# One chain of 16 batches for the scan of four head pairs, with TensorE and loads in the source's order

## The chip, the cores and the metric

The kernel runs on one core of a Trainium2 chip. The metric is the device time of one execution in microseconds (us); a kernel's time is the median of its runs.

## The reference, cut to what matters

The reference is a two-layer trunk on 512 latent and 256 context tokens (768 together), width 1024. The first layer mixes by a recurrent scan (RWKV-7, in both directions) next to a windowed attention, the second by two attentions; each has an MLP behind it. Every sub-layer is modulated by a vector made from `c` and a large matrix `w_ada`. The change is in the scan and in that modulation:

```python
def rwkv7_scan(f, d, s0, reverse):
    def step(state, inp):
        r_t, w_t, k_t, v_t, kk_t, a_t = inp
        sa = jnp.einsum('bhvk,bhk->bhv', state, -kk_t)
        state = (state * w_t[:, :, None, :] + sa[..., None] * (kk_t * a_t)[:, :, None, :]
                 + v_t[..., None] * k_t[:, :, None, :])
        return state, jnp.einsum('bhvk,bhk->bhv', state, r_t)
...
        ml = jnp.split(s_lat @ w_ada[i] + b_ada[i], 6, axis=-1)
        mc = jnp.split(s_ctx @ w_ada[i] + b_ada[i], 6, axis=-1)
```

The scan has 8 heads of 64 and two directions `d`; a step's state is a 64 x 64 matrix for each head. Weights and activations are float32.

## The kernel before

The kernel treats the scan in chunks of 64 tokens, 12 chunks in each direction (`NCH`), and the 8 heads as 4 pairs `p`; both heads and both directions of a pair share each instruction's 128 partitions.

**Preparation.** `prep(p)` (L842) is a generator for one pair; each `yield` is a turn. It loads k and r, normalises (`heads_rstd`, L397), makes decays (L864 matmuls, L872 and L874 running sums), and stops at FRONT. Then it makes the factors `BK` and `AR` (L897 to L942) and a triangular matrix for each chunk (L911, L912), which goes through DRAM (`nscr`, L919, L922) into a layout in which VectorE inverts its 32 x 32 blocks by 31 rank-one updates (L948, L949: "the doubling" below); READY stands before these. The result goes through DRAM again (L953 to L961), MERGE stands there, and 192 small matmuls join the blocks (L968, L976) into `XI`. The tiles of pairs p and p+2 are the same buffers.

**The chain.** `chunks(p)` (L983) works on batches of `NB` = 3 chunks, four to a pair. For batch b: `factors` (transposes L1017, L1023, value matmuls L1031), `masked` (L1043, L1050), `own` (L1059), `solved` (L1068, which needs `XI`), `local` (L1080, L1093), `passed` (L1101 to L1107, giving MQ), and three `step`s (L1122, L1124, L1129), of which each needs the state of the one before. The loop at L1132 puts the first four of batch b between the last ones of batch b-1. A pair's chain is filled and drained on its own; it ends with the copy of `y` (L1158), which `mix_out` (L1161) turns into the pair's output.

**The modulation.** `ada` (L333) takes the 24 column blocks of `w_ada` of both layers; four are done earlier, 20 in this stage. A block is four loads of 512 KB (L341, three buffers), each used by 8 matmuls with 32-row stationary operands (L352, 16 instructions in the profile), then a copy to SBUF (L358), a summing transpose (L361) and an addition (L363).

**What sets the order.** For each pair the loop at L1468 takes the chain's turns; after each it takes `RATE3` turns of the background `behind` (the next pair's preparation, the previous pair's output, and the front of the pair after) and `RATE4` turns of `ada`:

```python
            for _ in cg:
                n += 1
                due[0] += RATE3
                due[1] += RATE4
                while due[0] >= 1:
                    due[0] -= 1
                    next(bg, None)
...
            for t in itertools.chain(bg, rest()):
                due[1] += RATE5
```

What is left of the background runs in `rest` before the next pair's chain begins. In this stage that is the order of the source only: a planner in the framework places every instruction on its engine by priority and by when it expects the operands, and so fixes each engine's queue before the program runs. The stage before (`tc.manual_schedule(engines=ORDERED)`, L1322) is one that keeps the source's order. PSUM is split here into two tiles of two banks (`wide`, for nearly everything), two banks for `y`, one for the state update `pd` and one for the modulation.

Of the kernel before, what the change touches and what calls it, by code (L numbers as in the profile page):

```python
# [28 lines left out]
RATE1, RATE2, RATE3, RATE4, RATE5 = 2.0, 1.5, 1.8, 0.7, 0.5  # L29
QUIET = "quiet"  # L30
FRONT = "front"
READY = "ready"
# [22 lines left out]
for _name, _w in [("ident", 128), ("bones", 128), ("cent", 128), ("ones", 1), ("bo2", 2), ("mab", 64), ("mr", 384), ("i2", 64),  # L55
                  ("mhalf", 12), ("sel", 8), ("tri", 256)]:
    CON[_name] = slice(_n, _n + _w)
    _n += _w
# [3 lines left out]
def constants():  # L62
# [12 lines left out]
    con[:, CON["mr"]] = np.concatenate([np.tile(s <= t, (1, 3)), np.tile(s + t <= 63, (1, 3))], 1)  # L75
# [12 lines left out]
    con[:, CON["sel"]] = (p[:, None] // 32 == np.arange(8)[None] // 2) & (p[:, None] % 32 == np.arange(8)[None] % 2)  # L88

# [86 lines left out]
def trunk(ctx: ExitStack, tc: tile.TileContext, xT, cT, vec_d, wada, we, wo_in, wout, wf1, wf2, lw2_d, la2_d, lg2_d,  # L176
# [188 lines left out]


# [30 lines left out]
    def heads_rstd(pl, x, n, ops, out, name="t0", bufs=2, **k):  # L397
# [3 lines left out]
        act(sq[:, :n], x, AF.Square, **k)  # L401
        pc = one()
# [6 lines left out]
        yield  # L409
        rx = pl.tile([128, 12, 64], F32, name=name, bufs=bufs)  # L410
        V.tensor_copy(rx[:, :2 * nt, :], r12[:, :2 * nt].unsqueeze(2).to_broadcast([128, 2 * nt, 64]))
        pb = wide()
# [429 lines left out]
    def prep(p, R, rt, iv, sts, res):  # L842
# [10 lines left out]
        yield from heads_rstd(rt, k, T, lambda o, i: ts(o, i, 1e-24, None, op0=ALU.max), pb, "t", NT0, scale=VV["kk"][:, p:p + 1])  # L853
# [88 lines left out]
        stt(kds, kds, VV["rk"][:, p:p + 1], r, op0=ALU.mult, op1=ALU.mult)  # L942
        yield READY
# [18 lines left out]
        res[p] = (AR, BK, XI, wc, kds)  # L962
# [20 lines left out]
    def chunks(p, y, ct, pch, res):  # L983
# [5 lines left out]
        AR, BK, XI, wc, kds = res[p]  # L989
# [3 lines left out]
        v = ct.tile([128, T], F32, name="v")  # L993
        nc.sync.dma_start(v, scr[3 + 3 * p + 2])
        py = pch.tile([128, 2, 512], F32, name="py")
        pd = pch.tile([128, 128], F32, name="pd")
        yp = py[:, :, 0:384].rearrange("p h (c f) -> p h c f", f=64)
        B = [{} for _ in range(NCH // NB)]
        last = None
        env = {}  # L1000

        def chain(*a, **k):

            nonlocal last
            if last is None:
                last = PE.matmul(*a, **k)
            else:
                with tc.issue_after(last.ins):
                    last = PE.matmul(*a, **k)  # L1009

        def factors(b):

            pt = wide()[:, 0:NB * 256].rearrange("p (x h k) -> p h x k", x=2 * NB, h=2)
            BT = B[b]["BT"] = ct.tile([128, 2, 2 * NB, 128], F32, name="BT", bufs=2)
# [4 lines left out]
            XA = B[b]["XA"] = ct.tile([128, NB, 2, 128], F32, name="XA", bufs=2)  # L1019
            pw = wide()  # L1020
# [3 lines left out]
            pv = pw[:, 512:512 + NB * 128].rearrange("p (i f) -> p i f", i=NB)  # L1024
            vr = ct.tile([128, NB, 64], F32, name="vr", bufs=2)
# [6 lines left out]
            act(XA[:, :, :, 64:128], pt)  # L1032
# [4 lines left out]
        def masked(b):  # L1037
# [412 lines left out]
    with ExitStack() as p2:  # L1450
# [9 lines left out]
        for t in early:  # L1460
            if t != QUIET:
                next(ag, None)
# [408 lines left out]
```

## Time and profile before

| | |
|---|---|
| time, median of 3 runs | 2070.47 us (2069.14 to 2079.63) |
| profiled execution | 2079.02 us, its span 2077.2 us |
| mean granted TensorE clock over the span | 0.964 |
| busy over the span: PE, PEld | 1940.1, 1663.0 us |
| busy over the span: DVE, ACT, POOL | 1116.6, 816.4, 115.2 us |

PE is TensorE's matmuls, PEld its loads of stationary operands, DVE VectorE, ACT ScalarE, POOL GpSimd, SPq the queue of SyncE, which issues most loads. Times in rows are microseconds from the span's start unless marked ns. The profiled execution is one of the kernel's executions and lies at the upper end of the runs. The granted clock is 1.0 or 0.5 (2.4 or 1.2 GHz) at each moment; a row shows its mean.

### The profile page before, as it was taken

How to read it: one execution, taken by the hardware profiler on the slowest of the kernel's cores; microseconds unless marked ns; L12 is line 12 of the kernel's file. 1: busy time of each engine (PE TensorE's matmuls, PEld its weight loads, DVE VectorE, ACT ScalarE, POOL GpSimd, SP SyncE). 2: the span in 40 equal slices, each digit the busy share in tenths (PEclk: the TensorE clock that was granted, in tenths of full speed). 3: DMA queues.
4: the chain of work that ended last, by engine and by line, in shares of the span. 5: the costliest groups of instructions: out<-in, count | busy, mean ns of one | idle time of the engine just before them, and what ended most of it. 6: DMA issues, size and time to landing. Idle time of an engine off the chain costs nothing.

```text
span 2077.2 us, 40236 instructions
## 1 busy us (share of the span) xinstructions
PE 1940.1 (93%) x17276; PEld 1663.0 (80%) x17276; DVE 1116.6 (54%) x1991; ACT 816.4 (39%) x1531; POOL 115.2 (6%) x129
## 2 busy tenths in 40 slices
PE   6999996889879899999999999899999899999997
PEld 4788774676667797888888889898878798888887
DVE  5576567546454468234443444765565566444445
ACT  3466432434325344413221232445686645322232
POOL 1000011001000000000000000001121000000000
PEclk9999997798979999999999999999999999999998
DMA  7421335575643234312221221333111425332221
GB/s 308 154 84 62 108 96 138 186 224 165 187 150 109 78 97 132 102 41 82 72 61 41 72 82 41 101 112 100 37 42 41 133 92 163 102 92 82 88 95 41
DMA packets 112019, 217.64 MB, mean 105 GB/s; under 512 B 38496, under 2 KB 63968, under 8 KB 111328
## 3 DMA queue, kind: packets, MB, share of 16 engines
q1 hardware_dynamic: 96544, 191.73, 29.3%
q10 hardware_dynamic: 15296, 23.33, 3.2%
q8 instruction: 135, 2.21, 0.5%
q14 instruction: 44, 0.36, 0.1%
HBM read 184.36 MB, written 28.05 MB: 102 GB/s over the span
## 4 chain that ended last, share of the span: by engine, by line
PE 73%; DVE 12%; issue 5%; ACT 4%; DMA 4%; POOL 2%; SPq 0%; POOLq 0%; ACTq 0%; DVEq 0%
PE x L1568 43%; PE x L429 11%; PE ax L529 3%; PE ax L510 2%; PE b L492 2%; PE b L493 1%; PE b L1009 1%; PE ad L352 1%; DVE X L949 1%; DMA w_raw<-in_wada_dram 1%; DVE pr L948 1%; PE b L1068 1%; DVE w_lo L226 1%; POOL r L265 1%; DMA w_raw<-in_wf_dram 1%
## 5 line engine op out<-in xcount | busy, mean ns | idle before, releaser
L183 ACT ACTIVATE w_hi<-w_raw 128x1024 fp32r<-128x1024 f32 x183 | 192.3, 1057 | 482.1 <-PE x L1568 361.0
L226 DVE TENSOR_TENSOR w_lo<-w_raw,w_hi 128x1024 fp32r<-128x1024 f32 x181 | 220.9, 1224 | 204.3 <-ACT w_hi L183 203.4
L1568 PE MATMUL x<-fl,w_hi 128*128 128x256 f32 (+1 forms) x864 | 291.6, 339 | 3.9 <-DVE fl L1655 3.9
L1568 PE MATMUL x<-fh,w_lo 128*128 128x256 f32 (+1 forms) x864 | 290.1, 337 | 0.0
L1568 PE MATMUL x<-uh,w_hi 128*128 128x512 f32 (+1 forms) x864 | 287.1, 338 | 3.0 <-ACT uh L183 2.9
L1568 PE MATMUL x<-ul,w_hi 128*128 128x512 f32 (+1 forms) x864 | 287.8, 336 | 0.0
L1568 PE MATMUL x<-uh,w_lo 128*128 128x512 f32 (+1 forms) x864 | 287.4, 335 | 0.0
L1568 PE MATMUL x<-fh,w_hi 128*128 128x256 f32 (+1 forms) x864 | 287.4, 338 | 0.0
L1582 DVE TENSOR_TENSOR oa<-x,oa 128x512 f32<-128x512 f32 (+1 forms) x184 | 103.1, 563 | 207.6 <-PE x L1568 206.9
L429 PE MATMUL x<-uh,w_hi 128*128 128x256 f32 (+1 forms) x560 | 189.6, 339 | 0.9 <-ACT po L183 0.6
L429 PE MATMUL x<-uh,w_lo 128*128 128x256 f32 (+1 forms) x560 | 188.3, 336 | 0.0
L429 PE MATMUL x<-ul,w_hi 128*128 128x256 f32 (+1 forms) x560 | 188.1, 336 | 0.0
L1568 PEld LDWEIGHTS x<-fl,w_hi 128*128 128x128 f32 x864 | 165.2, 191 | 22.0 <-DVE fl L1655 4.5
L1568 PEld LDWEIGHTS x<-fh,w_lo 128*128 128x128 f32 x864 | 164.9, 191 | 17.8
L1568 PEld LDWEIGHTS x<-uh,w_hi 128*128 128x128 f32 x864 | 161.9, 190 | 21.3 <-ACT uh L183 4.0
L1568 PEld LDWEIGHTS x<-fh,w_hi 128*128 128x128 f32 x864 | 162.7, 191 | 19.9 <-ACT fh L183 2.5
L1568 PEld LDWEIGHTS x<-ul,w_hi 128*128 128x128 f32 x864 | 162.7, 189 | 17.7
L1568 PEld LDWEIGHTS x<-uh,w_lo 128*128 128x128 f32 x864 | 162.7, 189 | 17.6
L429 PEld LDWEIGHTS x<-uh,w_hi 128*128 128x128 f32 x560 | 106.8, 191 | 10.1 <-ACT po L183 0.8
L429 PEld LDWEIGHTS x<-uh,w_lo 128*128 128x128 f32 x560 | 106.9, 191 | 9.7 <-issue 1.7
L429 PEld LDWEIGHTS x<-ul,w_hi 128*128 128x128 f32 x560 | 106.8, 191 | 9.1 <-issue 1.2
L1654 DVE TENSOR_TENSOR rl<-rl 128x512 f32<-128x512 f32 (+1 forms) x108 | 59.4, 551 | 72.2 <-ACT fh L183 72.0
(303 smaller groups left out, 3441.8 us busy)
## 6 DMA issues: line engine op xcount, KB each, us to landing
w_raw<-in_wf_dram SPq DMA_DIRECT2D x128, 512.0 KB
w_raw<-in_wada_dram SPq DMA_DIRECT2D x96, 512.0 KB
w_raw<-in_we_dram SPq DMA_DIRECT2D x21, 512.0 KB
w_raw<-in_wo_in_dram SPq DMA_DIRECT2D x18, 512.0 KB
w_raw<-in_wout_dram SPq DMA_DIRECT2D x16, 512.0 KB
hsc<-h ACTq DMA_DIRECT2D x8, 1024.0 KB
scr<-po ACTq DMA_DIRECT2D x21, 384.0 KB
h<-hsc SPq DMA_DIRECT2D x7, 1024.0 KB
```

The costliest lines, as they stand in the source:

```text
L183: return S.activation(o, i, f, **k)
L226: eng.tensor_tensor(o_lo, x, o_hi.bitcast(F32), op=ALU.subtract)
L265: G.tensor_tensor(dst, src, C["mhalf"][:, :n], op=ALU.pow)
L352: PE.matmul(ps[32 * j:32 * j + 32, 0:128], si[:, 2 * kp + k, :], w[:, k, j * 128:(j + 1) * 128], start=kp + k == 0, stop=kp == 3 and k == 1)
L429: PE.matmul(ps[:, 0:b - a], x, y, start=j == 0, stop=j == len(pairs) - 1)
L492: PE.matmul(ps[:, off:off + n], qs, kh, start=True, stop=False)
L493: PE.matmul(ps[:, off:off + n], qs, kl, start=False, stop=True)
L510: PE.transpose(pt[:, (kb - k0) * 128:(kb - k0 + 1) * 128], P[:, kb * 128:(kb + 1) * 128], ident)
L529: PE.matmul(po[h * 64:h * 64 + 64, 0:128], v(h, k), pts[h][:, k], start=k == 0, stop=k == n - 1)
L1568: PE.matmul(o, a, b, start=n == 0, stop=n == len(pairs) - 1)
L1582: tt(oa[:, m, tok], ps, oa[:, m, tok], op=ALU.add)
L1654: tt(r, r, r, op=ALU.mult)
```

## The change

The four chains become one generator `batches` over 16 batches g = 4p + b: in each iteration it works on batches g-1 (`given`, the steps), g (`begun`, `gained`, `passed`, first step) and g+1 (`factors`, `values`, `masked`, `own`, `solved`), also across the border of two pairs. `local` is cut in `gained` and `given`, `passed` in `begun` and `passed`, `factors` in `factors` and `values`. From the stage's `manual_schedule` on, TensorE and SyncE take their instructions in the source's order; the other engines are still planned. Three PSUM tiles of two banks serve everything but `y`; the state update and the modulation take theirs from them. `Ada` handles half blocks: four loads of 256 KB (six buffers) and one `run` of 16 matmuls, whose four 32-row bands keep the two k halves apart, and `turn` sums them with `sel4`. A run stands at each SIDE, two in an iteration, a `turn` at TURN. The background goes on by 1.4 turns after each named turn and is finished at MERGE, before the first `solved` of the next pair; six turns are added in `heads_rstd` of each preparation, and `mix_out` waits in its generator until its `y` is made.

```diff
-RATE1, RATE2, RATE3, RATE4, RATE5 = 2.0, 1.5, 1.8, 0.7, 0.5
+RATE1, RATE2, RATE3 = 2.0, 1.5, 1.4
...
+    class Ada:
+
+
+
+        def __init__(self, wa, which, eng):
+            self.wa, self.eng, self.got, self.rows = wa, eng, [], []
+            self.which = [(l, q, h) for l, q in which for h in range(2)]
+            self.todo = [wada[l, q, kp][:, :, 256 * h:256 * h + 256] for l, q, h in self.which for kp in range(4)]
+
+        def load(self, n):
+            while self.todo and len(self.got) < n:
+                w = self.wa.tile([128, 2, 256], F32, name="w_half")
+                self.eng.dma_start(w, self.todo.pop(0))
+                self.got.append(w)
+
+        def run(self, n):
+            if not self.which:
+                return
+            ps = wide()[:, 0:128]
+            for kp in range(4):
+                w = self.got.pop(0)
+                for k in range(2):
+                    for j in range(2):
+                        b = 32 * (2 * k + j)
+                        PE.matmul(ps[b:b + 32], si[:, 2 * kp + k, :], w[:, k, j * 128:(j + 1) * 128], start=kp == 0, stop=kp == 3)
+            self.load(n)
+            rows = sp.tile([128, 128], F32, name="adar", bufs=2)
+            act(rows, ps)
+            self.rows.append((rows, self.which.pop(0)))
+
+        def turn(self):
+            if not self.rows:
+                return
+            pt = wide()
+            for n, (rows, _) in enumerate(self.rows):
+                PE.matmul(pt[:, 4 * n:4 * n + 4], rows, C["sel4"], start=True, stop=True)
+            for n, (_, (l, q, h)) in enumerate(self.rows):
+                m = slice(4 * q + 2 * h, 4 * q + 2 * h + 2)
+                tt(mod[:, l, m, :], pt[:, 4 * n:4 * n + 4].rearrange("p (a b) -> p a b", b=2),
+                   VV[f"bada{l}"][:, m].unsqueeze(2).to_broadcast([128, 2, 2]), op=ALU.add)
+            self.rows = []
+
...
+        for _ in range(slow):
+            yield
         pc = one()
...
+        for _ in range(1 + slow):
+            yield
...
-        yield from heads_rstd(rt, k, T, lambda o, i: ts(o, i, 1e-24, None, op0=ALU.max), pb, "t", NT0, scale=VV["kk"][:, p:p + 1])
+        yield from heads_rstd(rt, k, T, lambda o, i: ts(o, i, 1e-24, None, op0=ALU.max), pb, "t", NT0, 2, scale=VV["kk"][:, p:p + 1])
...
-            pw = wide()
+            XA = B[g]["XA"] = ct.tile([128, NB, 2, 128], F32, name="XA", bufs=2)
+            pw = B[g]["pw"] = wide()
...
-            pv = pw[:, 512:512 + NB * 128].rearrange("p (i f) -> p i f", i=NB)
...
+            act(XA[:, :, :, 64:128], pt)
+            v = tile_of(g)["v"]
+            vr = B[g]["vr"] = ct.tile([128, NB, 64], F32, name="vr", bufs=2)
             c0 = BWD[NB * b + NB - 1]
             act(vr[:, ::-1, ::-1], c3(v)[:, c0:c0 + NB])
+
+        def values(g):
+            p, b = divmod(g, nb)
+            v, vr, pw = tile_of(g)["v"], B[g]["vr"], B[g]["pw"]
+            pv = pw[:, 512:512 + NB * 128].rearrange("p (i f) -> p i f", i=NB)
...
-            Z = B[b]["Z"] = ct.tile([128, NB, 2, 2, 64], F32, name="Z", bufs=2)
+            Z = B[g]["Z"] = ct.tile([128, NB, 2, 2, 64], F32, name="Z", bufs=2)
...
+            if b == nb - 1 and p < 3:
+                values_in(p + 1)
...
-            tt(B[b]["BT"][:, :, :, 64:128], pr, C["mr"].rearrange("p (x t) -> p x t", t=64).unsqueeze(1).to_broadcast([128, 2, 2 * NB, 64]), op=ALU.mult)
...
+            for d in range(2):
+                x = slice(d * NB, d * NB + NB)
+                tt(B[g]["BT"][:, :, x, 64:128], pr[:, :, x], C["mr"][:, 64 * d:64 * d + 64].unsqueeze(1).unsqueeze(1).to_broadcast([128, 2, NB, 64]), op=ALU.mult)
...
+            BT, Z = B[g]["BT"], B[g]["Z"]
+            b = g % nb
+            if not b:
+                py = pch.tile([128, 2, 512], F32, name="py")
+                tile_of(g)["y"] = py[:, :, 0:384].rearrange("p h (c f) -> p h c f", f=64)
+            yp = tile_of(g)["y"]
...
+        def begun(g):
+
+            p, b = divmod(g, nb)
+            AR = res[p][0]
             i0 = 0 if b else 1
             pm = wide().rearrange("p (d x) -> p d x", d=2)[:, :, 0:NB * 128].rearrange("p d (i k) -> p d i k", i=NB)
             for d in range(2):
-                chain(pm[:, d, i0:, 0:64], ident, C["i2"].unsqueeze(1).to_broadcast([128, NB - i0, 64]), start=True, stop=False)
-                chain(pm[:, d, i0:, 64:128], ident, AR[:, NB * b + i0:NB * b + NB, 2 + d], start=False, stop=False)
+                PE.matmul(pm[:, d, i0:, 0:64], ident, C["i2"].unsqueeze(1).to_broadcast([128, NB - i0, 64]), start=True, stop=False)
+                PE.matmul(pm[:, d, i0:, 64:128], ident, AR[:, NB * b + i0:NB * b + NB, 2 + d], start=False, stop=False)
+            B[g]["pm"] = pm
...
+            MQ = B[g]["MQ"] = ct.tile([128, 2, NB, 128], F32, name="MQ", bufs=2)
...
             if s < NCH - 1:
+                pd = wide()[:, 0:128]
...
+            if s == NCH - 1:
+                act(y.rearrange("p c (h f) -> p h c f", h=2), yp)
+                done_y.append(g // nb)
+
+        values_in(0)
+        for g in range(-1, 4 * nb + 1):
+            old, now, new = 0 < g, 0 <= g < 4 * nb, g + 1 < 4 * nb
+            work = [old and (given, g - 1), new and (factors, g + 1), now and (begun, g), TURN, new and (values, g + 1), now and (gained, g),
+                    new and (masked, g + 1), now and (passed, g), SIDE, new and (own, g + 1),
+                    old and (step, g - 1, 1), SIDE, old and (step, g - 1, 2), new and (solved, g + 1), now and (step, g, 0)]
+            for w in filter(None, work):
+                if w in (SIDE, TURN):
+                    yield w
+                    continue
+                if w[0] is solved and not w[1] % nb:
+                    yield MERGE
+                w[0](*w[1:])
+                yield (w[0].__name__, w[1])
...
-        sts[1], ct, tl, wa = side("st1"), side("ct"), side("tl"), side("wa", 3)
-        p2.enter_context(psum(0, 2))
+        sts[1], ct, tl, wa = side("st1"), side("ct"), side("tl"), side("wa", WH)
+        p2.enter_context(psum(0, 3))
         pch = p2.enter_context(pool("pch", 1, space=PSUM))
-        pad = p2.enter_context(pool("pad", 1, space=PSUM))
-        mk = lambda: pad.tile([128, 512], F32, name="ad")
-        ag = ada(wa, 3, mk, [(0, q) for q in range(4, 12)] + [(1, q) for q in range(12)], nc.sync)
+        ag = Ada(wa, [(0, q) for q in range(4, 12)] + [(1, q) for q in range(12)], nc.sync)
+        ag.load(WH)
         y = tl.tile([128, 6, 128], F32, name="y")
-        for t in early:
-            if t != QUIET:
-                next(ag, None)
+        for n, t in enumerate(early):
+            if t != QUIET and n % 4 == 0:
+                ag.turn()
+                ag.run(WH)
         gate = mix_gate(tl)
...
+        def behind(p):
+
+            def out():
+                if p:
+                    while p - 1 not in done_y:
+                        yield QUIET
+                    yield from mix_out(p - 1, y, gate, tl, res)
+            if p < 3:
+                if p:
+                    yield from until(preps[p + 1], READY)
+                yield from turns(until(preps[p + 1], MERGE), out(), front(p + 2))
+                yield from preps[p + 1]
+                return
+            yield from out()
...
+        p2.enter_context(tc.manual_schedule(engines={mybir.EngineType.PE, mybir.EngineType.SP}))
         for t in until(preps[1], READY):
-            next(ag, None)
+            pass
         for t in preps[0]:
-            next(ag, None)
-        for p in range(4):
-            cg, n = chunks(p, y, ct, pch, res), 0
-
...
-            due = [0.0, 0.0]
-            t = None
-            for _ in cg:
-                n += 1
-                due[0] += RATE3
-                due[1] += RATE4
-                while due[0] >= 1:
-                    due[0] -= 1
-                    next(bg, None)
-                while due[1] >= 1:
-                    due[1] -= 1
-                    next(ag, None)
...
+        done_y = []
+        bgs = [behind(p) for p in range(4)]
+        due, p = 0.0, 0
+        for t in batches(y, ct, pch, res, done_y):
+            if t == SIDE:
+                ag.run(WH)
+            elif t == TURN:
+                ag.turn()
+            elif t == MERGE:
+                if p:
+                    for _ in bgs[p - 1]:
+                        pass
+                p += 1
+            elif p:
+                due += RATE3
+                while due >= 1:
+                    due -= 1
+                    next(bgs[p - 1], None)
+        for _ in bgs[3]:
+            pass
+        while ag.which or ag.rows:
+            ag.run(WH)
+            ag.turn()
+        mk = wide
         end = mix_last(3, y, tl, p3w["last"], p3w["gate"], mk)
```

## Rows read from the trace of the kernel before

**Rows 1.** The page's first part: busy time, share of the span, instructions.

```profile
PE 1940.1 (93%) x17276; PEld 1663.0 (80%) x17276; DVE 1116.6 (54%) x1991; ACT 816.4 (39%) x1531; POOL 115.2 (6%) x129
```

**Rows 2.** Windows of the stage: length, busy time by engine, PEclk, DMA share, GB/s.

```profile
330.00:368.00 38.00, 19.96 (x440) 15.55 (x444) 24.55 (x48) 10.69 (x21) 7.23 (x5) 0.66 0.78 217
368.00:717.00 349.00, 302.91 (x6254) 238.95 (x6245) 178.35 (x384) 133.77 (x253) 24.59 (x15) 0.89 0.51 156
...
576.00:655.00 79.00, 65.09 (x1418) 52.84 (x1417) 40.19 (x98) 26.05 (x55) 3.62 (x2) 0.87 0.35 103
655.00:717.00 62.00, 53.65 (x1074) 44.01 (x1075) 28.73 (x39) 30.37 (x52) 2.28 (x1) 0.93 0.35 114
...
690.00:712.00 22.00, 20.67 (x505) 18.44 (x496) 6.43 (x12) 6.81 (x14) 0.00 (x0) 1.00 0.08 27
```

**Rows 3.** Chain of waits: start, length, what; one operation at both clocks.

```profile
449.58 0.57 PE ad L352 x16
...
465.48 1.01 PE ad L352 x16
```

**Rows 4.** Timeline of one batch of pair 3: start, length, instruction.

```profile
695.97 0.29 DVE L1124 TENSOR_TENSOR x<-pd,Nb 128x128 f32<-128x128 f32 x1 [1.31 <-PE pd L1122]
...
698.67 0.49 ACT L183 ACTIVATE XA<-b 128x384 f32<-128x384 f32 x1 [0.33 <-PE b L1031]
699.18 0.98 ACT L183 ACTIVATE Z<-b 64x384 f32<-64x384 f32 x2
...
700.87 0.56 DVE L1044 TENSOR_TENSOR AK<-b,con 128x384 f32<-128x384 f32 x1 [3.74 <-PE b L1043]
701.59 0.96 DVE L1051 TENSOR_TENSOR BT<-b,con 128x768 f32<-128x768 f32 x1 [0.17 <-PE b L1050]
703.93 0.96 DVE L1107 TENSOR_TENSOR MQ<-b,wc 128x768 f32<-128x768 f32 x1 [1.39 <-PE b L1009]
...
707.10 0.29 DVE L1124 TENSOR_TENSOR x<-pd,Nb 128x128 f32<-128x128 f32 x1 [1.31 <-PE pd L1122]
```

**Rows 5.** Waits of TensorE, 310 to 740: total us, times, longest.

```profile
PE b L968 <- DMA xw<-tscr: 9.4, 2, 7.9
PE ad L352 <- DMA w_raw<-in_wada_dram: 8.0, 10, 2.0
PE ad L352 <- DVE mod L363: 7.8, 4, 4.1
PE pd L1122 <- DVE MQ L1107: 5.7, 8, 2.3
```

**Rows 6.** TensorE by line, 368 to 717: busy us, mean ns, idle before.

```profile
L352 PE MATMUL ad<-w_raw,si 128*32 128x128 f32 x1136 | 52.4, 308 | 13.8 <-DVE mod L363 7.5 <-DMA w_raw<-in_wada_dram 6.0
...
L361 PE MATMUL ad<-con,adar 128*128 128x8 f32 x36 | 6.9, 265 | 0.5 <-ACT adar L183 0.4
```

**Rows 7.** Chain of waits: loads of the modulation.

```profile
439.77 4.35 DMA w_raw<-in_wada_dram
...
453.58 5.49 DMA w_raw<-in_wada_dram
```

**Rows 8.** Chain of waits: the projection before the stage.

```profile
299.83 14.61 PE x L429 x87
```

**Rows 9.** Preparation of pair 2: VectorE's timeline, then the chain of waits.

```profile
436.37 0.96 DVE L902 TENSOR_TENSOR bk<-t,ei 128x768 f32<-128x768 f32 x1 [0.62 <-PE b L1050]
...
485.63 0.18 DVE L948 TENSOR_TENSOR pr<-X,N 96x31 f32<-96x31 f32 x1
...
523.88 1.06 DVE L952 COPY N<-X 96x1024 f32<-96x1024 f32 x1
...
354.58 3.09 DMA tscr<-N
...
567.83 1.00 PE b L968 x29
```

**Rows 10.** Waits of SyncE's queue, 330 to 720.

```profile
SPq L953 <- DVE X L949: 26.8, 4, 12.2
```

More of the change, by code (lines that the diff above doesn't have):

```diff
@@ L27 @@
 EM05 = math.exp(-0.5)
-RATE1, RATE2, RATE3, RATE4, RATE5 = 2.0, 1.5, 1.8, 0.7, 0.5
+RATE1, RATE2, RATE3 = 2.0, 1.5, 1.4
 QUIET = "quiet"
 FRONT = "front"
+SIDE = "side"
+TURN = "turn"
 READY = "ready"
@@ L942, in prep @@
         stt(kds, kds, VV["rk"][:, p:p + 1], r, op0=ALU.mult, op1=ALU.mult)
+        res[p] = (AR, BK, XI, wc, kds)
         yield READY
@@ L981, in trunk, with batches @@
     NB = 3
-    def chunks(p, y, ct, pch, res):
-        AR, BK, XI, wc, kds = res[p]
+    WH = 6
+    def batches(y, ct, pch, res, done_y):
         half = lambda q: slice(q * 64, q * 64 + 64)
@@ L992, in chunks, with tile_of, values_in, factors @@
         ch = (FWD, BWD)
[L993 to L1011, printed above, removed]
+        nb = NCH // NB
+        B = [{} for _ in range(4 * nb)]
+        tiles = {}
+        def tile_of(g):
+            p = g // nb
+            if p not in tiles:
+                tiles[p] = dict(X=None)
+            return tiles[p]
+        def values_in(p):
+            v = ct.tile([128, T], F32, name="v")
+            nc.sync.dma_start(v, scr[3 + 3 * p + 2])
+            tile_of(p * nb)["v"] = v
+        def factors(g):
+            p, b = divmod(g, nb)
+            AR, BK, XI, wc, kds = res[p]
             pt = wide()[:, 0:NB * 256].rearrange("p (x h k) -> p h x k", x=2 * NB, h=2)
-            BT = B[b]["BT"] = ct.tile([128, 2, 2 * NB, 128], F32, name="BT", bufs=2)
+            BT = B[g]["BT"] = ct.tile([128, 2, 2 * NB, 128], F32, name="BT", bufs=2)
             for d in range(2):
@@ new lines, in behind @@
+        def behind(p):
[11 more added lines that the diff above has]
+            yield from out()
+            for x in mixs[::-1]:
+                x.close()
+            p3w["W"] = ffstream(p3w["x"].enter_context(pool("wp3")), 0)
+            m0 = p3w["m0"] = p3w["m"].enter_context(pool("m0"))
+            p3w["last"] = m0.tile([128, T], F32, name="last")
+            yield from bonus(3, tl, res, gate, p3w["last"])
+            mh = m0.tile([128, KT, 256], F32R, name="mh")
+            ml = m0.tile([128, KT, 256], F32R, name="ml")
+            p3w["mh"] = mh, ml
+            for j in range(8):
+                for _ in range(3):
+                    yield
+                p3w["W"].ahead(j + 1)
+                if j in (5, 6):
+                    a, b = ((4, 8), (0, 3))[j - 5]
+                    if a:
+                        mr = m0.tile([128, 4, 256], F32, name="mr")
+                    else:
+                        mr = tl.tile([128, T], F32, name="t", bufs=2).rearrange("p (k t) -> p k t", k=3)
+                    nc.sync.dma_start(mr, mixd[a:b, :, 0:256].rearrange("k p t -> p k t"))
+                    split(mh[:, a:b], ml[:, a:b], mr)
```

162 lines of the change are left out of this document (46 added, 116 removed).

## Prediction

> **What bounds the kernel now.** I read the page's head first: TensorE (PE) is busy 93% of the span and no other engine over 54% [rows 1]. So the change must win time where TensorE is not fully used, and the windows by stage show that this is the stage it rewrites. Its first batch starts at 368 us and its last ends at 717. In these 349 us TensorE is busy 302.9, VectorE 178.4 and ScalarE 133.8, and the mean granted clock is 0.89 [rows 2]. TensorE alone is near its limit, and it loses in two ways: 46.1 us idle, and a clock that falls. A mean of 0.89 between the levels 1.0 and 0.5 is 22% of the stretch, 77 us, at the lower one. The chain of waits has the same work at both levels: 16 modulation matmuls take 0.57 us and 1.01 us [rows 3], a ratio of 1.77. With a busy share of 0.75 in such stretches (an estimate, below the stage's 0.87), the low clock costs about 77 x 0.75 x (1 - 1/1.77) = 25 us. Idle and low clock together are 71 us: the most that a better order can bring back.
>
> Where they arise is seen by pairs. Pair 2 (576 to 655) has 65.1 busy of 79 and a clock of 0.87, pair 3, with no preparation beside it, 53.7 of 62 and 0.93; in the middle of pair 3, 690 to 712, it is 20.7 of 22 at the full clock [rows 2]. There one batch takes 11.13 us, from one state update to the same one a batch later [rows 4]. The loss sits at the joints between pairs, where a chain drains, merges are awaited and the next chain fills.
>
> **The change part by part.** The sum starts from 71 us and takes off what the new program gives back or adds.
>
> One chain over all pairs: three of four fills and drains go, since the factors of pair p+1 run beside the last steps of pair p. The work per batch stays: the same transposes, `masked`, `passed`, `solved`, steps. `masked` writes the second mask in two VectorE instructions for one of 0.96 us [rows 4]; VectorE has 171 us idle in the stretch, and its evictions are awaited three TensorE groups later, so nothing. `res` set earlier and the narrower constants: nothing, no engine works for them.
>
> Source order on TensorE and SyncE. An instruction that waits now holds whatever stands behind it in the source, also background work that could run. The waits that are seen before TensorE today are of the kinds that the new order moves apart: for MQ 5.7 us, the modulation's PSUM 7.8, its loads 8.0, the merge's transfer 9.4 [rows 5]. MQ is now first read after both SIDE runs, `own` and `solved`, some 5 us after `passed`, against 0.96 us of VectorE [rows 4]. What is left per iteration I count as 0.67 us (the idle time of an undisturbed batch, 22 minus 20.67 over two batches, rows 2), plus about 0.45 for the loads and 0.4 for background evictions (below): 1.5 us. From iteration -1 to 16 there are 18, so 27 us. Below, the work is so well spread that 0.5 us stay (9); above, each iteration loses what a batch loses now, 71 / 16 = 4.4 us (80).
>
> Three shared PSUM pairs. Per iteration the chain takes about 13 (two in `factors`, two in `masked`, one each in `begun`, `gained`, `own`, `solved`, TURN, two SIDE, two steps), the background some 4. `begun` holds one until `passed`, `factors` one until `values`, so for that time one turns alone. Evictions take 0.49 to 0.98 us [rows 4]; 17 tiles held some 2 us each over three buffers are 11 us. An iteration's TensorE work is more: 10.5 for a batch (11.13 less 0.67), 2.3 for two runs, 0.8 for their transposes, and for the background 4.2 (302.9 busy, less 25 for the clock, 16 x 10.5 for batches and 59 for the modulation, over twelve iterations), together near 18. A background tile that meets the held one waits for about one eviction: 0.4 us an iteration, from 0 to 0.98.
>
> The modulation. The matmuls stay (128 columns, 32-row bands, 16 per 512 KB); in the stretch they are busy 52.4 us [rows 6]. The four bands now carry the two k halves as well, so the closing transpose sums them, and there is one for each half: 20 more, at 6.9 us for 18 pairs of instructions [rows 6], 0.38 us each: 7.7 us on TensorE, hidden by nothing while TensorE is the bound. Twenty more VectorE additions and ScalarE copies lie beside it. Forty halves meet 36 places in the chain, and the remaining four are run in `early`, every fourth turn; a half left over would cost its run, copy, transpose and addition in series at the end, about 3 us (0 to 12 for four; I take 0).
>
> Its loads. Six buffers of 256 KB are as much as three of 512. SyncE can issue a new load only when a run has freed its buffer, and the second SIDE stands only `own` and one step behind the first. From the first buffer freed to the third tile needed there are about 3/4 of a run (1.0 us), `own` (0.9), a step (0.4), three background turns (0.7, at 4.2 for 17) and half a run (0.6): 3.6 us, for the fourth 3.9. Loads in the chain of waits took 4.35 and 5.49 us, for twice the bytes and with another in flight [rows 7]. So a wait of 0 to 1.9 us an iteration; I take 0.45, by the shorter row. Bandwidth is no bound: the share of the DMA engines is 0.51 [rows 2], and the modulation's 71 loads are 37 of the 54 MB moved; if its now four times shorter pieces took double time, the share would be 0.86. The Trainium skill (DMA: Bandwidth & Descriptors, "Measured") speaks against the cut: it asks for transfers of 1 MiB and over, since about 2.0 us of each are fixed. By its formula a half would take 2.6 us and a whole 3.2; no row here shows a 256 KB load of this kind. By that price alone the loads would be in time and the wait zero, 8 us better than mine; by its rule on size the stage would move less per second, which matters only if the share reaches 1.
>
> The background. RATE3 falls from 1.8 to 1.4 a turn, but a pair has 48 named turns for 37: 67 steps for 66, while a middle pair needs about 69 with the six turns added to `heads_rstd`. It just fits; the last two are drained at MERGE. These turns also stand before pair 0's doubling in `early`, at 1.5 a column step: four steps of eight matmuls, at 14.61 us for 87 [rows 8], are 5.4 us later. VectorE is full only in part of 330 to 368 (24.6 of 38, rows 2), so between 0 and 5.4; I take 2. The first iterations have nothing to lie beside: values, `own` and `solved` wait for evictions of 0.98, 0.56, 0.49 and 0.98 us and their queues: 5 us, from 3 to 8.
>
> Sum: 71 - 27 - 7.7 - 2 - 5 = 29 us. The profiled execution took 2079.0 us, 1.8 of them outside its span, and would take 2050. It is 8.5 above the median of the runs shown, 2070.5; as nothing says that this difference goes, I subtract from the median: 2041 us.
>
> **The rivals.**
> A. *The order hides nearly all.* Waits of 0.5 us an iteration, no late load: 18 us better, and with the small waits inside a batch's 11.13 us gone too, 2008 to 2022. For it: the undisturbed batches hold the full clock at 94% busy [rows 2]. Against: background and modulation were not in them.
> B. *Preparation sets the pace.* Pair p+1 can't be built before pair p-1 has given back its tiles, so from MERGE to MERGE there must be room for factors, a transfer, the doubling and the merge. Before, one such passage took 131 us: the first `bk` at 436.4, doubling 485.6 to 523.9, merge at 567.8 [rows 9]. Much of it was waiting for its turn; back to back I count 9 for the factors (nine of an iteration's 17 turns), 12 for four transfers at 3.1, 38 for the doubling, 1 for its copy and 7 for 192 merge matmuls at 1.00 for 29 [rows 9]: 67 us against 4 x 18 = 72. If it takes 100, the two middle pairs take 200 for 144 and the gain is gone, less what the other engines do meanwhile: no change, 2060 to 2080. TensorE, in order, would stand at the merges.
> C. *The head of the queue blocks: slower.* In source order SyncE waits at the store of the doubled matrix, and the modulation's loads stand behind it; it waited 26.8 us at that line in four pairs, up to 12.2 [rows 10]. Then the second SIDE stops TensorE and with it the chain. With the longer load (5.49 us) each iteration waits 1.9 us, 1.4 over mine, 26 us; three times 6.7 us at the store that TensorE sees in full are 20, and the clock falls again in the gaps, up to the 25 us of today: 71 us against a gain of 29: 2112, and from 29 us on it is no gain, from 40 slower. The Trainium skill (PSUM — Partial Sum Buffer, "Engine vs sequencer instructions") says that matmuls start and complete in program order; the waits in [rows 5] agree. By it nothing may pass a blocked run, which is this case's mechanism. For it: the short distance between the two SIDE turns. Against: one and a half runs are loaded ahead.
>
> **How the numbers follow.** Forecast 0.50 (own range 2022 to 2060: waits of 0.5 to 2.5 us an iteration), A 0.15, B 0.16, C 0.19. Half a per cent, about what a measurement here can tell from no change, is 10 us: 2060 to 2081. So faster 0.65, same 0.16, slower 0.19. The range, 2008 to 2092, leaves out the far end of C and a little beyond A.
>
> **What would show it.** Right: from the first transposes to the last y the stage takes about 320 us for 349, its clock is 0.97 or more, no joint between pairs is seen in TensorE's busy share, and the modulation is busy until the last iteration. The load term is wrong if TensorE's waits for the half blocks exceed 10 us in total; the PSUM term, if waits for evictions before the background's matmuls exceed 8. B would show as waits before the merge matmuls of over 10 us a pair, C as a SyncE wait at the store followed by TensorE waiting for half blocks. The prediction falls if the stage takes over 340 us, or if the time moves outside it.

## The result and the profile after

The changed kernel takes 2135.60 us, the median of 4 runs (2132.72 to 2139.75), against 2072.10 for the kernel before in the same comparison: ratio 1.0302, 95% interval 1.0267 to 1.0338. It is 3% slower; the forecast was 2041, with an upper end of 2092. The profiled execution took 2132.7 us, its span is 2130.9 (2077.2 before), its mean clock 0.950 (0.964).

The page's first part, as [rows 1]: TensorE's busy time is what it was (1940.1 before). All 54 us are time in which it is not busy.

```profile
PE 1939.3 (91%) x17316; PEld 1669.3 (78%) x17316; DVE 1122.0 (53%) x2027; ACT 820.3 (38%) x1551; POOL 113.0 (5%) x129
```

Windows of the kernel after, with the columns of [rows 2]: the part before the stage, the stage, and then the stage's passages, each from the first `solved` of one pair to the first `solved` of the next (the last one ends with the last `y`).

```profile
330.00:374.00 44.00, 18.11 (x347) 13.11 (x341) 31.23 (x61) 14.38 (x26) 7.71 (x5) 0.50 0.46 116
374.00:764.00 390.00, 301.10 (x6331) 245.23 (x6331) 178.15 (x407) 136.76 (x271) 25.05 (x15) 0.85 0.47 144
386.00:466.10 80.10, 67.00 (x1484) 55.78 (x1482) 37.31 (x83) 35.90 (x73) 5.22 (x4) 0.91 0.47 141
466.10:566.60 100.50, 79.58 (x1662) 64.03 (x1654) 57.11 (x128) 37.93 (x75) 11.73 (x7) 0.88 0.45 130
566.60:672.10 105.50, 72.73 (x1631) 60.52 (x1626) 43.11 (x112) 26.63 (x59) 5.82 (x3) 0.81 0.41 116
672.10:763.40 91.30, 70.15 (x1375) 55.54 (x1371) 31.06 (x59) 31.57 (x56) 2.28 (x1) 0.84 0.61 203
```

From the first transposes to the last `y` the stage takes 388.7 us (374.7 to 763.4) against 347.2 before (369.0 to 716.2): +41.5. It starts 5.7 later, and what follows the last `y` is 6.5 longer (1367.5 for 1361.0). Together that is the 53.7 us between the two spans. TensorE idles 88.9 us in the stage for 46.1, and the clock fell from 0.89 to 0.85 where it was to rise to 0.97.

TensorE's waits inside the stage (total us, times, longest). [rows 5] shows a wider window of the kernel before: its 9.4 us for the merge's transfer all lie before 368 us, at the merge of pair 0. Between 368 and 717 the kernel before has no such wait, and its loads make 6.0 us:

```profile
PE ad L352 <- DMA w_raw<-in_wada_dram: 6.0, 9, 1.5
```

In the kernel after, from 374 to 764, the loads have grown to 37.5 and the merge from nothing to 21.5:

```profile
PE b L393 <- DMA w_half<-in_wada_dram: 37.5, 28, 7.8
PE b L1018 <- DMA xw<-tscr: 21.5, 6, 11.9
PE b L1145 <- DVE mod L407: 5.7, 2, 2.8
PE b L404 <- ACT xw L186: 2.1, 2, 1.1
PE b L1104 <- ACT Z L186: 1.9, 5, 0.4
```

How one of the waits for loads comes about: SyncE's timeline in the kernel after (start, length, instruction), then TensorE's in the same place (in brackets the wait before it).

```profile
477.03 2.11 SPq L969 DMA_DIRECT2D nscr<-XI  x4
481.19 0.31 SPq L972 DMA_DIRECT2D N<-nscr  x1
481.60 4.82 SPq L381 DMA_DIRECT2D w_half<-in_wada_dram  x7
```

```profile
480.39 0.64 PE L393 MATMUL b<-w_half,si 128*32 128x128 f32 x16
485.39 0.43 PE L393 MATMUL b<-w_half,si 128*32 128x128 f32 x8 [4.36 <-DMA w_half<-in_wada_dram]
```

SyncE stands at the stores of the triangular matrices until VectorE has made `XI`, then at the load of `N`; the half blocks whose buffers are free come behind, and TensorE, at the run, lets nothing pass. In the last pair the output's weights are ahead of them in the queue. The loads resume at 732.65 and TensorE has waited 7.79 us:

```profile
720.24 7.50 SPq L242 DMA_DIRECT2D w_raw<-in_wout_dram  x3
727.79 0.43 SPq L1572 DMA_DIRECT2D mr<-mixd  x1
...
732.65 2.51 SPq L381 DMA_DIRECT2D w_half<-in_wada_dram  x4
```

```profile
737.45 0.66 PE L393 MATMUL b<-w_half,si 128*32 128x128 f32 x8 [7.79 <-DMA w_half<-in_wada_dram]
```

The end, on TensorE's timeline: half blocks, their sums, and only then the output. The output's first matmul stands 7.6 us behind the last `y`; before, it was at 715.27, ahead of `y` (though its stream then stopped for 3.2 us).

```profile
762.50 2.65 PE L393 MATMUL b<-w_half,si 128*32 128x128 f32 x32
765.08 1.54 PE L404 MATMUL b<-con,adar 128*128 128x4 f32 x6
768.47 1.69 PE L1294 MATMUL b<-con,y 128*128 128x128 f32 x6 [1.85 <-DVE y L1291]
771.00 0.58 PE L1638 MATMUL x<-mh,w_hi 128*128 128x256 f32 x1 [0.84 <-DVE last L1295]
```

### The profile page after: what moved, and what is told of

Read it like the earlier page. It is cut to its first block, busy times and chain, and to the rows that moved or that the text cites. A ratio compares the mean times of both kernels' runs of the same rounds, so it can differ in the third digit from the quotient of the medians.

```text
span 2130.9 us, 40583 instructions
## 1 busy us (share of the span) xinstructions
PE 1939.3 (91%) x17316; PEld 1669.3 (78%) x17316; DVE 1122.0 (53%) x2027; ACT 820.3 (38%) x1551; POOL 113.0 (5%) x129
## 4 chain that ended last, share of the span: by engine, by line
PE 74%; DVE 9%; DMA 6%; issue 4%; ACT 4%; POOL 2%; SPq 1%; POOLq 0%; ACTq 0%; DVEq 0%
PE x L1638 44%; PE x L479 10%; PE ax L579 3%; DMA w_half<-in_wada_dram 3%; PE ax L560 2%; PE b L542 2%; PE b L543 1%; PE b L393 1%; PE b L1133 1%; DVE X L1000 1%; POOL r L268 1%; DVE pr L999 1%; PE b L914 1%; PE b L1111 1%; DMA tscr<-N 1%
## 5 line engine op out<-in xcount | busy, mean ns | idle before, releaser
L1638 PEld LDWEIGHTS x<-ul,w_hi 128*128 128x128 f32 x864 | 162.4, 189 | 17.7
```

The lines of the kernel that those rows point to most:

```text
L1638: PE.matmul(o, a, b, start=n == 0, stop=n == len(pairs) - 1)
```

## The experiments

Three causes were to be told apart: half blocks that come late, the fixed order itself (SyncE's, TensorE's), and the merge, which the background reaches before the chain needs it. The medians of the kernel before were 2072.3 to 2073.3 us in all comparisons.

**The fixed order, taken back in two steps.**

```diff
-        p2.enter_context(tc.manual_schedule(engines={mybir.EngineType.PE, mybir.EngineType.SP}))
+        p2.enter_context(tc.manual_schedule(engines={mybir.EngineType.PE}))   # sp_planned; all_planned: no line
```

> SyncE alone is given back to the planner; TensorE stays in the source's order. Theory L (the half blocks come late because SyncE, in order, stands before other transfers): the waits of the modulation's matmuls for loads fall from 37.5 us to under 15 and the time from 2135 to about 2105. Rival M (the merge of the next pair is due too early for its preparation, 21 us of waits inside the stage): loads and time change by less than 10 us. Rival O (TensorE's own fixed order loses what the planner filled): about 2130.

> Both queues are given back to the planner, the chain of 16 batches, shared PSUM and half blocks stay. Theory L: as with SyncE alone, about 2105. Rival M: waits before the merge fall as the planner puts other work first, about 2110. Rival O: the whole loss was the fixed order, 2075 or below.

sp_planned: 2124.67 us, ratio 1.0245 (1.0219 to 1.0270), stage 382.8. all_planned: 2099.06, 1.0113 (1.0083 to 1.0142), stage 351.9, clock 0.89. SyncE's order costs about 11 us, TensorE's about 26 more. The rest of the change still costs 1.1%. Neither time is one that was expected: with SyncE planned the load waits in the stage fall only to 27.5 us, and 2099 lies between theory L and rival O. Of all_planned's waits in the stage one for the merge takes 18.6 us, and the loads make 15.8.

**The fixed order alone, in the kernel before.**

```diff
+        p2.enter_context(tc.manual_schedule(engines={mybir.EngineType.PE, mybir.EngineType.SP}))
         for t in until(preps[1], READY):
             next(ag, None)
```

> The kernel before with one edit: TensorE and SyncE take the source's order from the same point on. Its four chains, its PSUM and its whole blocks stay. Theory L: whole blocks have more time, so at most 2090. Rival O: the fixed order costs by itself, 2110 or more. Rival M: merges stand at the end of a pair, after all of its background, so 2072 to 2100.

2113.13 us, ratio 1.0182 (1.0153 to 1.0211). Its longest waits of TensorE, from 300 to 720 us, are loads again, and the modulation's PSUM tile, held until VectorE comes round; the merge is not among them.

```profile
PE ad L352 <- DMA w_raw<-in_wada_dram: 38.8, 14, 10.2
PE ad L352 <- DVE pr L948: 17.1, 1, 17.1
PE ad L352 <- DVE mod L363: 10.3, 16, 2.9
```

So with 512 KB loads and a PSUM bank of the modulation's own, the order alone costs 41 us, as rival O expected. It doesn't cost them all where the kernel after does: the 17.1 us are one wait before the stage, which begins 17.7 us later (386.7). The stage takes 366.4 us, 19.2 more than before, and TensorE idles 76.6 in it.

**The loads: another queue, another place, another size.** loads_pool issues them from GpSimd's queue; spread puts the first SIDE behind TURN, so that the two runs stand half an iteration apart; whole loads 512 KB (three buffers), two for a run, and closes with two accumulated `sel` matmuls.

```diff
-        ag = Ada(wa, [(0, q) for q in range(4, 12)] + [(1, q) for q in range(12)], nc.sync)
+        ag = Ada(wa, [(0, q) for q in range(4, 12)] + [(1, q) for q in range(12)], nc.gpsimd)   # loads_pool
...
-  ... now and (begun, g), TURN, new and (values, g + 1), ... now and (passed, g), SIDE, new and (own, g + 1),
+  ... now and (begun, g), TURN, SIDE, new and (values, g + 1), ... now and (passed, g), new and (own, g + 1),   # spread
...
-            for kp in range(4):
+            for i in range(2):
+                w, kp = self.got.pop(0), 2 * self.which[0][2] + i      # whole: w is [128, 2, 512]
                 for k in range(2):
-                    for j in range(2):
+                    for j in range(4):
```

> The modulation's half blocks of this stage are issued from GpSimd's queue instead of SyncE's; all else as after. Theory L: what stands before them on SyncE no longer delays them, nor they the preparation; load waits under 12 us, about 2100. Rival M and rival O: 2130 or more, since neither the merge nor TensorE's order is touched.

> After, with the first modulation run of an iteration moved from behind passed to just behind TURN, so that the two runs stand about half an iteration apart; as many runs, buffers and loads. Theory L (a run follows the other within one load time): load waits from 37.5 us to under 15, time 2110 to 2118. If SyncE standing still is the cause rather than the short distance, waits stay over 25 and the time within 8 us of 2135.

> After, but each run takes two whole loads of 512 KB (three buffers) in place of four halves, and one summing transpose pair closes a block; same places in the order, same matmuls. If the cut into halves is a cause (160 issues of 0.56 us on SyncE for 80 of 0.33): load waits under 25 us and 2115 to 2125. If only place and order matter: within 8 us of 2135.

loads_pool is no better: 2146.65 us, 1.0349 (1.0322 to 1.0376), load waits in the stage 34.2 us. spread takes the wait away and gains little: 2129.03, 1.0285 (1.0257 to 1.0313). Inside the stage TensorE waits 7.4 us for half blocks instead of 37.5, but its waits from 300 to 720 now begin so:

```profile
PE b L1018 <- DMA xw<-tscr: 40.5, 8, 18.8
PE b L404 <- DVE t L1245: 19.7, 2, 9.9
```

The first row is hardly new (38.4 in the kernel after, in the same window). The second is: TURN waits for a PSUM tile that `mix_out` holds. whole: 2129.07, 1.0284 (1.0254 to 1.0315), load waits 35.5. That half blocks are late is true. But another queue or size leaves them late, and spread, which doesn't, brings a wait of its own; the best of the three gains 7 us, and its interval overlaps that of the kernel after. What late loads alone cost is not shown by these runs.

**The modulation left out.** SIDE and TURN do nothing, and the loop that runs the half blocks left behind the chain goes too.

```diff
-            if t == SIDE:
-                ag.run(WH)
-            elif t == TURN:
-                ag.turn()
+            if t in (SIDE, TURN):
+                pass
```

> After without the modulation's runs and summing transposes in the chain and behind it: 36 of the 40 half blocks are left out of the computation. Theory L: runs and transposes (64 us busy) and their load waits go, but the merge waits stay and grow, since the preparation now sets the pace: 2060 to 2075. If the preparation were far from the bound, the stage would lose all of the 100 us: 2035 or below.

2062.44 us, ratio 0.9949 (0.9932 to 0.9967), as theory L expected. The windows of this kernel, the four passages:

```profile
383.30:447.20 63.90, 53.71 (x1206) 45.48 (x1208) 38.34 (x77) 32.88 (x63) 5.25 (x4) 0.95 0.13 30
447.20:537.50 90.30, 70.28 (x1393) 57.92 (x1389) 54.74 (x116) 35.64 (x66) 11.52 (x7) 0.81 0.18 48
537.50:630.20 92.70, 59.42 (x1356) 51.83 (x1350) 41.81 (x100) 24.33 (x50) 5.91 (x3) 0.76 0.17 42
630.20:695.20 65.00, 51.09 (x1027) 43.58 (x1021) 28.96 (x46) 28.39 (x46) 2.27 (x1) 0.92 0.34 117
```

In the two middle passages TensorE idles 20.0 and 33.3 us without the modulation, and 20.9 and 32.8 with it; in the whole stage 78.7 and 88.9. So the half blocks don't use that idle time, they are added to it: the two passages get shorter by 10.2 and 12.8 us without them, about as much as TensorE has less to do there (9.3 and 13.3). But it is the sum that stays, not what it is made of. These are the waits of the second of the two passages, first in the kernel after, then in no_mod:

```profile
PE b L1018 <- DMA xw<-tscr: 13.8, 2, 11.9
PE b L393 <- DMA w_half<-in_wada_dram: 11.2, 8, 4.4
```

```profile
PE b L1019 <- DMA xw<-tscr: 23.8, 2, 21.6
```

Over both passages 19.3 us of load waits go, and the merge's grow from 17.4 to 32.1: a chain that its loads don't delay comes to the merge sooner and waits there. Without the modulation only the first and the last passage run near the forecast's pace (64 and 65 us; 18 us an iteration less 2.3 for two runs and 0.8 for their transposes make 60), and there it costs 16 and 26 us.

**The merge held until the chain asks for it.**

```diff
-                yield from preps[p + 1]
+                while p + 1 not in held:      # MERGE adds p to held
+                    yield QUIET
+                yield from preps[p + 1]
```

> After, with the merge of the next pair held back until MERGE, one batch later in TensorE's order; nothing else moves. Theory M: the waits of the merge matmuls inside the stage (about 21 us of the 38) fall under 6, time 2115 to 2120. Theory L: the loads stay as late, 2130 or more.

> The merge held until MERGE and both queues given back to the planner. all_planned took 2099 and waited some 20 us for one merge inside the stage; theory M: without it 2078 to 2084, still not under before, since two more transposes an iteration and the later start stay. If the planner fills that wait with other work already: 2095 or more.

hold: 2114.64 us, 1.0210 (1.0170 to 1.0249): 21 us gained with both engines in order, close to what theory M expected. The merge's waits in the stage are gone, and those for the loads have grown from 37.5 to 45.4. hold_planned, without `manual_schedule`: 2071.16, 0.9993 (0.9976 to 1.0009), 28 us better than all_planned, better than expected and equal to the kernel before. Windows of hold_planned, the stage and the 22 us behind it:

```profile
374.00:700.00 326.00, 293.68 (x6251) 236.50 (x6250) 172.82 (x403) 133.94 (x269) 26.50 (x15) 0.92 0.55 164
700.00:722.00 22.00, 20.29 (x171) 17.06 (x172) 8.78 (x19) 5.78 (x13) 2.27 (x1) 0.77 0.64 202
```

With the merge held and a planned order the stage takes 326 us, 21 less than before: 14 less idle time and 7 less busy time, of which 4.3 are two runs that now stand behind the last `y`. The start is 4.5 us later, and what follows the last `y` is 9 us longer. That leaves 7 us between the two profiled executions, and 2 between the medians, inside the interval.

Pairs of runs that differ only in who orders TensorE and SyncE price the fixed order at 37 us (the kernel after against all_planned), 43 (hold against hold_planned), 36 (hold_spread against hold_spread_planned, below) and 41 (order_alone against the kernel before); holding the merge is worth 21 us in order and 28 planned. The two edits together take back all that the change lost.

**Combinations.** hold_spread has both edits in order; hold_spread_planned is the same without `manual_schedule`; hold_spread_rate20 is hold_spread with `RATE3` at 2.0, the background further ahead.

> Both single edits together: the merge held until MERGE, the two modulation runs half an iteration apart. If the two causes are separate and each hid the other, merge waits inside the stage stay under 6 us and load waits under 12, and the time falls by more than the sum of the single gains (20 and 6): 2095 to 2105. If the loads are late whatever the distance: 2108 or more.

> Merge held, runs apart, both queues planned: the three edits that each took something away. If the chain over all pairs has any gain left over four chains, it shows here: 2060 to 2075. If the preparation's length is the bound whatever the order: 2078 to 2090.

> hold_spread with RATE3 at 2.0 for 1.4: the preparation's turns come earlier in the source, the queues stay in order. Theory P (a preparation is paced by its turns and not by its work): VectorE starts the doubling some 8 us earlier in each pair, so any merge wait left goes, 3 to 10 us under hold_spread. If background turns in a row stop TensorE instead: 5 us or more over hold_spread.

2111.74 us (1.0196, 1.0168 to 1.0223), 2076.01 (1.0025, 1.0008 to 1.0043) and 2130.28 (1.0281, 1.0255 to 1.0306). The 3 us that spread adds to hold are inside the intervals, and hold_spread's expected 2095 to 2105 was missed: the merge's waits in the stage are gone and the loads' are 12.8 us, but TURN waits 19.7 for `mix_out`'s tile here too, and TensorE idles 81.0. hold_spread_planned falls between its two expected ranges. More background per turn is worse by 19 where theory P expected a gain. Preparation doesn't get quicker by it: from pair 2's first `bk` to its first masked triangle it takes 38.2 us, against 32.5 in hold_spread; why is open.

**Start and end of hold_planned.** hp_start takes the six added turns from pairs 0 and 1; hp_extra adds a SIDE in four iterations; hp_both does both.

```diff
-        yield from heads_rstd(rt, k, T, ..., pb, "t", NT0, 2, scale=VV["kk"][:, p:p + 1])
+        yield from heads_rstd(rt, k, T, ..., pb, "t", NT0, 2 if p > 1 else 0, scale=VV["kk"][:, p:p + 1])   # hp_start
...
-  now and (begun, g), TURN, new and (values, g + 1),
+  now and (begun, g), TURN, g in (2, 5, 8, 11) and SIDE, new and (values, g + 1),   # hp_extra
```

> The chain held at the merge and with the planner's order (hold_planned), and the six added turns of heads_rstd only for pairs 2 and 3, none for pairs 0 and 1. Theory: those of pair 1 stand before pair 0's doubling and made its last copy 4.5 us later (358.0 against 353.5). If so, the copy is back at 353.5 to 355, the first factors start 3 to 5 us earlier (near 369), the stage stays at 326 and the time falls by 3 to 5 us, to 2066 to 2068. Rival: the later start comes from the PSUM tiles shared with the modulation and its half blocks, so the copy stays at 357 to 359 and the time within 2 us of 2071.

> As hold_planned, with one SIDE more behind TURN in iterations 2, 5, 8 and 11 (three row buffers for two), so that the 37 half blocks left at the chain's start are through before its last iteration. Theory: the end is late because half blocks are left: in hold_planned five runs of 2.6 us at the lower clock lie behind 690 us, and the output's first matmul (mh) comes 9 us after the last y where it stood before it in the kernel before. With them gone the time behind the last y falls from 1370 to 1361 to 1365; the chain has four runs more in the middle, some 1.2 us each at the full clock, 5 us, of which idle time hides some: net 2 to 8 us faster, 2063 to 2069. Rival: the tail is set by the output's own VectorE chain (y, last), not by the runs; then it stays at 1368 to 1371 and the stage grows by 0 to 5 us: 2071 to 2076.

> Both edits. If start and tail are separate losses, their gains add: 2057 to 2066, faster than the kernel before by 0.3 to 0.7 per cent. If either rival holds, it is no better than the better one of the two.

2081.95 us (1.0034, 1.0017 to 1.0052), 2086.53 (1.0055, 1.0038 to 1.0072) and 2083.22 (1.0046, 1.0029 to 1.0064). Both local readings held, in profiled executions that lie 5 us above the median for hp_start and 7.5 below it for hp_extra. The copy that ends pair 0's doubling, VectorE's rows of the kernel before, of after and of hp_start (ns; the fourth field gives the start):

```profile
L952 DVE COPY N<-X x1: 1030/1030/1030, 353.5 to 353.5; 96x1024 f32<-96x1024 f32 x1
```

```profile
L1003 DVE COPY N<-X x1: 1031/1031/1031, 359.2 to 359.2; 96x1024 f32<-96x1024 f32 x1
```

```profile
L1003 DVE COPY N<-X x1: 1031/1031/1031, 353.0 to 353.0; 96x1024 f32<-96x1024 f32 x1
```

It went from 358.0 in hold_planned to 353.0, the first factors from 373.5 to 367.6; and in hp_extra what follows the last `y` fell from 1370.4 to 1364.9. The time followed neither, and the three expectations for it were missed: hp_start's stage grew to 336.6 us and its half blocks ran on until 721, hp_extra's grew to 336.1, hp_both's to 345.1. With the planner, which places every instruction anew after each edit, a gain at one end was given back at another. Why it comes back just there stays open. No version here beats the kernel before and keeps all of the work.

## Why the prediction was wrong

The step that failed is the term of 1.5 us an iteration for "an instruction that waits now holds whatever stands behind it": 27 us of waits, and with them a clock back near 1.0. It is made of small waits and has no place for a merge that comes before its preparation is done. That was put at nothing because the background's turns "just fit" (67 steps for 66), which counts turns and no time. In its place the runs show 36 to 43 us for the fixed order of the two engines, and 21 for the merge, which without the fixed order costs 28. Measured against the sum:

- *Idle time.* 27 + 5 = 32 us were forecast inside the stage, 88.9 measured, or 4.9 us for each of 18 iterations. My upper bound of 4.4, what a batch lost already, was below it, and the stage is far past the 340 us at which the prediction was to fall. I had counted waits inside an iteration (an eviction, a load) and none that spans iterations. The two middle passages, where preparation and chain meet in one queue, idle 53.7 us where eight iterations at 1.5 make 12. I had also taken the 9.4 us for the merge's transfer [rows 5] for a loss between pairs that the one chain removes; it lies before the stage.
- *The clock.* The 25 us for the low clock were booked as gain since the idle time was to go. It stayed, and the clock fell to 0.85; the stage's busy time is 301.1 for 302.9 and nothing came back. In the kernel after the passages with more idle time have the lower clock (13.1 us: 0.91; 32.8 us: 0.81).
- *Rival B, preparation sets the pace.* I gave it 0.16 and a price: 100 us for a middle passage instead of 72. It took 100.5 and 105.5. That they agree so well is partly luck, since waits for loads are in these passages too (19.3 us). My 67 us for a preparation, back to back, were too few: for pair 2 the first `bk` stands at 443.8, the last masked triangle at 476.9, the doubling from 484.9 to 526.0 and the merge at 544.0, so 33 us for the factors that I had put at 9, and 100 from the first to the last. The kernel before could have told: there the first masked triangle stands 22 us behind the first `bk`, here 28. That preparation isn't hidden shows in no_mod, whose middle passages take 90 and 93 us without the modulation, 32.1 us of them together waits for the merge. B's own test, merge waits above 10 us a pair, holds for one pair of three (11.9 + 1.9; 4.1 and 3.6 in the others): the rest of the price came as small waits and at the low clock, and how it divides among them stays open.
- *Rival C, the head of the queue.* It happens (477 to 485 us above), though at the stores of the triangular matrices and not at that of the doubled one. Its time, 2112, was nearest, and my range ended below it, at 2092. But C put 71 us on the late loads, the store and the clock in their gaps; giving SyncE's order back to the planner brings 11, and spreading the runs or whole loads bring 7 at most.
- *Loads.* 0.45 us an iteration, 8 us, were forecast, and over 10 would show it wrong: 37.5. The duration was right: the 15 half loads in the chain of waits took 3.15 to 5.11 us, around the 4.35 that I used [rows 7]. What was wrong is when they could start. The Trainium skill (DMA: Bandwidth & Descriptors, "Anatomy of one DMA — SWDGE (gpsimd) path") has a formula by which a half would take an estimated 2.6 us and a whole 3.2; it was fitted to loads that GpSimd issues, and the ones here are SyncE's. No half load in these chains was so quick, also not in that of loads_pool, where GpSimd issues them (3.49 to 5.62), and the thirteen 512 KB loads in the chain of whole took 3.39 to 6.08: the measurement decides, and by it a half costs about what a whole does.
- *Modulation and PSUM.* The runs cost what they did (52.8 us for 52.4 [rows 6]). The closing transposes cost 11.5 for 6.9, so 4.6 more, not 7.7. For PSUM, TURN waits 7.3 us for tiles held by others and the chain 5.7 for TURN's: 13 us, 0.7 an iteration for the 0.4 taken, inside the bounds given. Waits before the background's matmuls, which over 8 us were to show the term wrong, make under 4 where they are for an eviction. All this is read from waits alone; no run gives the modulation a bank of its own in the changed kernel.

```profile
L393 PE MATMUL b<-w_half,si 128*32 128x128 f32 x1172 | 52.8, 303 | 38.9 <-DMA w_half<-in_wada_dram 37.5 <-DVE MQ L1184 1.0 <-issue 0.2
L404 PE MATMUL b<-con,adar 128*128 128x4 f32 x70 | 11.5, 268 | 7.3 <-ACT xw L186 2.1 <-DVE XI L962 1.6 <-ACT BT L186 1.5
```

- *Start and end.* "Between 0 and 5.4; I take 2": 5.7, above the upper end, and hp_start, in a planned order, shows the added turns as the reason. A half block left at the end was put at about 3 us and its number at none: half blocks remain behind the last step (762.50 above), 4.2 us with their sums, and the output starts 7.6 us after `y`.

What came near is the stage of hold_planned: 326 us where I forecast 320, with 32 us idle as forecast, but a clock of 0.92. That is not a hit of the prediction, since in that kernel the order is planned and the merge held, and part of its work stands behind the last `y`. How much of its 21 us is the one chain's is not shown; no run has four chains with everything else as it is there.

## What to carry to other kernels

When an engine is put in the source's order, don't price each wait by its own length: take the work of which the order mixes two chains, and ask what each passage costs when neither may pass the other. Leave one stream of work out and look whether the idle time stays, and what it is then made of: here it was 53 us in the two middle passages with the modulation and without, which the modulation's waits (37.5 us, at the top of the list) would not have told. A wait at the top of the list whose removal gains little may stand in front of another: without the loads' waits the merge's grew, and with the merge held the loads' did.

## What the runs showed of the hardware

SyncE takes longer to issue a load that is cut: a half block of 256 KB 561 ns in the median, a whole of 512 KB 328. A half block's pieces are four times shorter (1 KB for 4 KB), and there are twice as many of them. The rows are SyncE's of the kernel after and of whole (ns, minimum, median, maximum).

```profile
L381 SPq DMA_DIRECT2D w_half<-in_wada_dram x142: 539/561/1918, 381.8 to 760.2; - x142
```

```profile
L381 SPq DMA_DIRECT2D w_half<-in_wada_dram x71: 327/328/623, 382.8 to 753.8; - x71
```

So 142 halves hold SyncE for about 80 us, 71 wholes for 23. Here it had the room: in the stage it waited 173 us for buffers that the runs free (the first row of its waits).

```profile
SPq L381 <- PE b L393: 173.0, 51, 19.4
SPq L1058 <- PE b L1089: 28.6, 3, 13.6
SPq L969 <- DVE XI L962: 19.7, 2, 9.9
```

The other two rows stand in the same queue ahead of half blocks: the next pair's `v`, which waits until `values` has read the last one, and the stores of the triangular matrices. At the store of the doubled matrix, where the prediction saw SyncE wait [rows 10], it waits 6.5 us in this stage.
